# The expert stage of an encoder block on one core, with its weight conversion pipelined by a step

## The chip, the cores and the metric

The kernel runs on one core of one Trainium2 chip. The metric is the device time of one execution in microseconds (us), lower being better. Engines are named as in the profile: PE multiplies matrices (PEld is its weight load), ACT and DVE are the scalar and the vector engine, POOL is GpSimd, SP issues most DMAs.

## What is computed

The block normalizes its input, runs a convolution branch and a bidirectional state-space branch, merges them, and adds a mixture of experts in which each of the 16 experts picks its 130 tokens. The change touches the mixture alone:

```python
def expert_choice_ffn(xn, w_router, w_gate, w_up, w_down):
    b, T, d = xn.shape                                   # 1, 1040, 1024
    cap = CAPACITY_FACTOR * T // N_EXPERTS               # 130
    aff = jax.nn.softmax(jnp.einsum('btd,de->bte', xn, w_router).astype(jnp.float32), axis=-1)
    top_aff, top_idx = lax.top_k(jnp.swapaxes(aff, 1, 2), cap)
    bi = jnp.arange(b)[:, None, None]
    xg = xn[bi, top_idx]
    hg = jnp.einsum('becd,edf->becf', xg, w_gate)        # w_gate, w_up: 16 x 1024 x 2048
    hu = jnp.einsum('becd,edf->becf', xg, w_up)
    y = jnp.einsum('becf,efd->becd', jax.nn.silu(hg) * hu, w_down)   # w_down: 16 x 2048 x 1024
    y = y * top_aff[..., None].astype(y.dtype)
    return jnp.zeros_like(xn).at[bi, top_idx].add(y)
```

## The kernel before

The expert stage is the last third of the program. It goes through 16 experts `e` in 4 steps `q` each, 64 steps in all. A step makes 512 of the 2048 hidden columns. It needs four weight tiles of 1 MB in float32, two of the gate (`m` = 0, halves `b` of the contraction) and two of the up matrix (`m` = 1), which `load_gu` (L898) brings into the pool `ring`; all of `ring`'s tiles are named `wst`.

The two products are made in float16 pieces. Per step `gate_up` does this:

- ACT squares the four tiles and sums each row (L912). The squares themselves are not used; they are written into the tile that is to hold `wl`. The sums go to `sq`.
- `scales` (L874 to L888) turns the sums into a power of two for each matrix: DVE rounds `sq` (`sqb`, L877), PE adds it over the partitions with two tiny products (L880), DVE makes the scales `sc` (L883 to L887).
- The weights are split: `wh` is the tile times its scale in float16, by ACT for `b` = 0 (L917) and by DVE for `b` = 1 (L918); `wl` is what `wh` leaves over, all four by DVE (L920). `wh` and `wl` live in the pool `split`.
- `pair(0)` and `pair(1)` each make 96 matmuls (`mm3`, L96 to L98: `wh` times the two pieces of the tokens `xT`, and `wl` times the first), then `sil` on ACT (L939) and `ac` on DVE (L941).

In the same step the previous expert's down product goes on: `bring` (L949) loads two tiles of `w_down` of 1 MB, and each `down` (L963) makes 16 float32 products of 8 column blocks out of one (in the profile 32 matmuls). After an expert's eighth `down` its result is copied (`yT`, L970), turned back by 16 transposes (L978), scaled (`yo`, L979) and added to memory by four indirect DMAs of POOL (L980): `put`. For the next expert, `Route` makes a one-hot table (L825), the list of tokens (`idx`, L837), gathers them with two indirect DMAs (L841), and `turn` transposes them (L869) into `xT` (ACT, L871). The first two steps of expert 0 take float32 weights (L931), and during the first experts `select` searches the threshold of the others.

The order on each engine comes out of a scheduler that takes the program's order as a priority; `high_priority(offset=...)` puts a piece ahead by so many instructions. All engines run their own list in order. A tile of a pool can be filled again when its last reader is through: `ring` has 10 tiles, `split` 8 `wh` and 8 `wl` (two steps' worth of four each), PSUM's `rp`, which the turns, the transposes of `put` and the norm product share, has two. The loads stand on SP in the order in which the program asks for them: gate and up of the next step, then the two down tiles of this one.

## Time and profile before

| what | us |
|---|---|
| median of 3 runs (lowest, highest) | 3150.16 (3142.86, 3152.40) |
| profiled execution | 3151.71 |
| its span | 3149.90 |
| PE busy | 2867.0 |
| DVE busy | 2208.8 |
| ACT busy | 1575.6 |
| POOL busy | 757.0 |
| expert steps, 1762.4 to 3085.3 of the span | 1322.9 |
| of these twelve experts, 1983.4 to 3011.2 | 1027.8 |

PE is busy in nine tenths of the span, but a busy PE can run at a lower clock: the column PEclk of the windows view is the clock that was granted, 1.00 being the upper one of two levels (2.4 GHz) and 0.50 the lower (1.2 GHz). So PE loses time in two ways, by standing idle and by a clock below 1.00, and both are read per stretch. A line in brackets in the waits and the timeline is the idle time before an instruction and what ended it. The DMA share is the busy share of the core's 16 DMA engines; it reads up to 1.05 where they are full.

### The profile page before, as it was taken

To read this page: it belongs to the slowest core of one execution; us is meant where nothing else is said; L and a number is where in the kernel's file an instruction comes from. 1 tells how busy PE (TensorE), PEld (TensorE's weight loads), DVE (VectorE), ACT (ScalarE), POOL (GpSimd) and SP (SyncE) were. 2 spreads that over 40 slices of the span, in tenths; PEclk is the share of its full clock that TensorE was granted. 3 is DMA by queue.
4 is the path that set the end of the run, shared out by engine and by line. 5 is a ranking of instruction groups with operands and counts; after the bars stand their busy time and mean duration, and the time that the engine had idled before them with its cause. 6 is when DMAs were issued, how large, how long until landed. Compare 5 with 4: busy or idle time off the path is not lost. (4 is left out here: it accounts for less than half of the span.)

```text
span 3149.9 us, 65509 instructions
## 1 busy us (share of the span) xinstructions
PE 2867.0 (91%) x28079; PEld 2716.6 (86%) x28079; DVE 2208.8 (70%) x2703; ACT 1575.6 (50%) x2351; POOL 757.0 (24%) x661
## 2 busy tenths in 40 slices
PE   8999999886987989899997888999999999999996
PEld 7999999776776778889966888999998999999996
DVE  7967769396896886897455766677776666666683
ACT  4423333443646464443222665665665656556653
POOL 1101011253454544330000003222222222221123
PEclk9999999898999899999998999999999999999998
DMA  4324233677768776524345778989888888888995
GB/s 119 108 91 136 78 119 104 170 140 197 142 198 164 205 162 157 173 61 133 119 135 204 265 272 294 319 312 331 304 303 287 306 297 308 305 310 307 318 341 161
DMA packets 425971, 665.99 MB, mean 211 GB/s; under 512 B 29217, under 2 KB 213953, under 8 KB 425673
## 3 DMA queue, kind: packets, MB, share of 16 engines
q1 hardware_dynamic: 366032, 514.83, 51.7%
q0 software_dynamic: 25760, 73.27, 7.6%
q10 hardware_dynamic: 33888, 73.71, 7.3%
q8 instruction: 220, 3.60, 0.5%
q14 instruction: 71, 0.58, 0.1%
HBM read 585.15 MB, written 76.59 MB: 210 GB/s over the span
## 5 line engine op out<-in xcount | busy, mean ns | idle before, releaser
L98 PE MATMUL gu<-xT,wl 128*128 128x130 f16 x3968 | 710.8, 223 | 50.4 <-DVE wl L920 50.4
L96 PE MATMUL gu<-xT,wh 128*128 128x130 f16 x3968 | 718.4, 226 | 17.6 <-ACT wh L917 15.5
L97 PE MATMUL gu<-xT,wh 128*128 128x130 f16 x3968 | 717.3, 223 | 0.0
L96 PE MATMUL mm<-uh,wh 128*128 128x346 f32 (+2 forms) x1752 | 583.9, 333 | 21.3 <-ACT wh L151 18.6
L97 PE MATMUL mm<-ul,wh 128*128 128x346 f32 (+2 forms) x1752 | 580.3, 331 | 0.3 <-DVE ul L187 0.3
L98 PE MATMUL mm<-uh,wl 128*128 128x346 f32 (+2 forms) x1752 | 579.2, 332 | 0.0
L920 DVE SCALAR_TENSOR_TENSOR wl<-wst,sc,wh 128x2048 f16<-128x2048 f32 x248 | 569.6, 2344 | 0.0
L912 ACT ACTIVATE wl<-wst 128x2048 bf16<-128x2048 f32 x248 | 470.5, 1899 | 180.0 <-PE gu L98 168.2
L963 PE MATMUL dn<-ac,wst 128*128 128x130 f32 x3840 | 473.7, 279 | 11.3 <-DMA wst<-in_w_exp_down_dram 11.2
L963 PEld LDWEIGHTS dn<-ac,wst 128*128 128x128 f32 x3840 | 447.1, 192 | 14.9 <-DMA wst<-in_w_exp_down_dram 14.9
L98 PEld LDWEIGHTS <-wl 128*128 128x128 f16 x3968 | 390.3, 99 | 54.8 <-DVE wl L920 54.8
L96 PEld LDWEIGHTS <-wh 128*128 128x128 f16 x3968 | 393.2, 99 | 20.7 <-ACT wh L917 20.1
L97 PEld LDWEIGHTS <-wh 128*128 128x128 f16 x3968 | 399.4, 101 | 3.3 <-issue 2.1
L96 PEld LDWEIGHTS mm<-uh,wh 128*128 128x128 f32 x1752 | 337.1, 192 | 36.6 <-ACT wh L151 20.2
L97 PEld LDWEIGHTS mm<-ul,wh 128*128 128x128 f32 x1752 | 337.1, 192 | 12.7 <-issue 11.7
L98 PEld LDWEIGHTS mm<-uh,wl 128*128 128x128 f32 x1752 | 336.3, 192 | 10.8 <-issue 10.4
L235 DVE SCALAR_TENSOR_TENSOR co<-ci,cp,co 128x1040 f32<-128x1040 f32 x240 | 344.1, 1434 | 1.7
L841 POOL DMA_INDIRECT xg<-hn_d,idx x32 | 151.2, 4725 | 767.9 <-DVE wgt L845 726.4
L917 ACT ACTIVATE wh<-wst,sc 128x2048 f16<-128x2048 f32 x124 | 241.4, 1994 | 88.7 <-DVE sc L885 74.8
L428 ACT ACTIVATE E<-row,cst 128x128 f32<-128x128 f32 (+1 forms) x576 | 170.1, 378 | 200.3 <-DMA row<-cs_d 162.9
L420 POOL TENSOR_TENSOR xw<-xk,dtw 128x512 f32<-128x512 f32 (+1 forms) x136 | 189.3, 1397 | 178.8 <-DMA xk<-xk_d 74.6
L151 ACT ACTIVATE wh<-wr 128x1024 fp32r<-128x1024 f32 (+1 forms) x113 | 105.6, 934 | 243.6 <-PE mm L97 194.4
(329 smaller groups left out, 4642.0 us busy)
## 6 DMA issues: line engine op xcount, KB each, us to landing
wst<-in_w_exp_gate_dram SPq DMA_DIRECT2D x128, 1024.0 KB, 8.2
wst<-in_w_exp_up_dram SPq DMA_DIRECT2D x128, 1024.0 KB, 10.4
wst<-in_w_exp_down_dram SPq DMA_DIRECT2D x128, 1024.0 KB, 7.9
wr<-in_w_in_dram SPq DMA_DIRECT2D x73, 512.0 KB, 4.4
row<-cs_d SPq DMA_DIRECT2D x64, 512.0 KB, 10.3
xk<-xk_d ACTq DMA_DIRECT2D x64, 256.0 KB, 6.3
xbc_d<-po POOLq DMA_DIRECT2D x24, 520.0 KB, 3.2
xk_d<-xt POOLq DMA_DIRECT2D x20, 512.0 KB, 3.9
```

The costliest lines, as they stand in the source:

```text
L96: pe.matmul(ps, wh(k), xh(k), start=(k == 0), stop=False)
L97: pe.matmul(ps, wh(k), xl(k), start=False, stop=False)
L98: pe.matmul(ps, wl(k), xh(k), start=False, stop=(k == K - 1))
L151: act.activation(out=wh[:, :K], in_=r, func=AF.Copy)
L235: dve.scalar_tensor_tensor(co, ci[:, m:m + T], cp[:, j, m:m + 1], co, op0=OP.mult, op1=OP.add)
L420: pool.tensor_mul(heads(o[:L]), heads(xk[:L]), dtw[:L, c, w, hs].unsqueeze(2).to_broadcast([L, HG, 64]))
L428: act.activation(out=E[:L, j, :L], in_=row[:L, j, :L], func=AF.Relu, scale=-1.0, bias=cs)
L841: self.got = nc.gpsimd.indirect_dma_start(out=xg.rearrange("p a d -> p (a d)"), out_offset=None, in_=hn_d.rearrange("t a d -> t (a d)"), i ...
L912: act.activation(out=wl[m][b].bitcast(BF), in_=t[m][b], func=AF.Square, accum_out=sq[:, b, m:m + 1])
L917: act.activation(out=wh[m][0], in_=t[m][0], func=AF.Copy, scale=sc[:, 1, m:m + 1])
L920: dve.scalar_tensor_tensor(wl[m][b], t[m][b], sc[:, 1, m:m + 1], wh[m][b], op0=OP.mult, op1=OP.subtract)
L963: pe.matmul(last["dn"][b // 3][:, b % 3], t[:, k, b * P:b * P + P], ac[:, 2 * i + k], start=(i + k == 0 and b % 3 == 0), stop=(i == 7 and ...
```

## The change

- The squares go into one tile of their own, `junk` (L762), which nobody reads, and no longer into `wl`. They are a function of their own, `norms`.
- Scales and split of step n+1 (`convert`) stand in the middle of step n, between its first `down` and its second pair. The scales' priority offset falls from 1500 to 150. A step's `gate_up` takes the finished tiles.
- Gate and up tiles are asked for two steps ahead and no longer one (`RUN`), after the step's two down tiles and no longer before them.
- `ring` has 11 tiles, not 10; `wh` has 7, not 8; `wl` has 6, not 8.
- `sil` and `ac` get a priority offset of 300, `yo` too.
- `put` is a generator: the first half of the result's columns starts at the end of the expert's last step and goes on after the next step's first pair, the second after its second pair.
- The next expert's `route` stands in step 1, no longer in step 0 (expert 2's was there already).

```diff
@@ -34,9 +34,9 @@
 NR = 2
 NS = NE - NR
 PRE = 2
-RUN = 1
+RUN = 2
 NATIVE = (0, 1)
-SELECT, LATE = 1, 1
+SELECT = 1
 NCH = [(0, 348), (348, 346), (694, 346)]
 NCH0 = [(0, 272), (272, 384), (656, 384)]
 OFF_Z, OFF_XBC, OFF_DT, OFF_GATE = 2048, 4096, 7168, 7232
@@ -754,11 +754,12 @@
     HC = CAP // 2
     mstack, rings, splits, fins = ExitStack(), ExitStack(), ExitStack(), ExitStack()
     with mstack:
-        ring = rings.enter_context(tpool("ring", bufs=10, side="right"))
-        split = splits.enter_context(tpool("split", bufs=8, side="right"))
+        ring = rings.enter_context(tpool("ring", bufs=11, side="right"))
+        split = splits.enter_context(tpool("split", bufs=7, side="right"))
         go = mstack.enter_context(tpool("go", bufs=2))
         mo = mstack.enter_context(tpool("mo", bufs=2))
         sel = mstack.enter_context(tpool("sel"))
+        junk = sel.tile([P, 4, 512], BF, name="junk")
         mps2 = mstack.enter_context(tpool("mps2", bufs=2, space=PSUM))
 
         def every(t):
@@ -900,25 +901,35 @@
                     ts.append(t)
             return ts[:2], ts[2:]
 
+        def norms(t):
+
+            sq = go.tile([P, 2, 2], F32, name="sq")
+            for m in range(2):
+                for b in range(2):
+                    act.activation(out=junk, in_=t[m][b], func=AF.Square,
+                                   accum_out=sq[:, b, m:m + 1])
+            return sq
+
+        def convert(t, sq):
+
+            with tc.high_priority(offset=150):
+                sc = scales(sq, sx[:, 0:1])
+            wh = [[split.tile([P, 4, 512], F16, name="wh") for _ in range(2)] for _ in range(2)]
+            wl = [[split.tile([P, 4, 512], F16, name="wl", bufs=6) for _ in range(2)] for _ in range(2)]
+            for m in range(2):
+                act.activation(out=wh[m][0], in_=t[m][0], func=AF.Copy, scale=sc[:, 1, m:m + 1])
+                dve.tensor_scalar_mul(wh[m][1], t[m][1], sc[:, 1, m:m + 1])
+                for b in (1, 0):
+                    dve.scalar_tensor_tensor(wl[m][b], t[m][b], sc[:, 1, m:m + 1], wh[m][b], op0=OP.mult,
+                                             op1=OP.subtract)
+            return wh, wl, sc
+
         def gate_up(t, q, xT, ac, first=None):
+
 
             native = first and q in NATIVE
             if not native:
-                wh = [[split.tile([P, 4, 512], F16, name="wh") for _ in range(2)] for _ in range(2)]
-                wl = [[split.tile([P, 4, 512], F16, name="wl") for _ in range(2)] for _ in range(2)]
-                sq = go.tile([P, 2, 2], F32, name="sq")
-                for m in range(2):
-                    for b in range(2):
-                        act.activation(out=wl[m][b].bitcast(BF), in_=t[m][b], func=AF.Square,
-                                       accum_out=sq[:, b, m:m + 1])
-                with tc.high_priority(offset=1500):
-                    sc = scales(sq, sx[:, 0:1])
-                for m in range(2):
-                    act.activation(out=wh[m][0], in_=t[m][0], func=AF.Copy, scale=sc[:, 1, m:m + 1])
-                    dve.tensor_scalar_mul(wh[m][1], t[m][1], sc[:, 1, m:m + 1])
-                    for b in (1, 0):
-                        dve.scalar_tensor_tensor(wl[m][b], t[m][b], sc[:, 1, m:m + 1], wh[m][b], op0=OP.mult,
-                                                 op1=OP.subtract)
+                wh, wl, sc = t
 
             def pair(p):
                 pss = []
@@ -934,11 +945,12 @@
                             mm3(ps[:, f], lambda k: wh[m][k // 4][:, k % 4, cols], lambda k: wl[m][k // 4][:, k % 4, cols],
                                 lambda k: xT[0][:, k], lambda k: xT[1][:, k], KD)
                     pss.append(ps)
-                sil = mo.tile([P, 2, CAP], F32, name="sil")
                 s0, s1 = (sx[:, 0:1], sx[:, 0:1]) if native else (sc[:, 2, 0:1], sc[:, 2, 1:2])
-                act.activation(out=sil, in_=pss[0], func=AF.Silu, scale=s0)
                 b0 = 4 * q + 2 * p
-                dve.scalar_tensor_tensor(ac[:, b0:b0 + 2], pss[1], s1, sil, op0=OP.mult, op1=OP.mult)
+                with tc.high_priority(offset=300):
+                    sil = mo.tile([P, 2, CAP], F32, name="sil")
+                    act.activation(out=sil, in_=pss[0], func=AF.Silu, scale=s0)
+                    dve.scalar_tensor_tensor(ac[:, b0:b0 + 2], pss[1], s1, sil, op0=OP.mult, op1=OP.mult)
 
             return pair
 
@@ -971,12 +983,14 @@
 
         def put(r):
             for b in range(2):
+                yield
                 yo = mo.tile([HC, 2, 512], F32, name=f"yo{b}", bufs=1)
                 for h in range(2):
                     ps = mps2.tile([HC, 4, P], F32, name="rp")
                     for j in range(4):
                         pe.transpose(ps[:, j], last["yT"][:, 4 * b + j, HC * h:HC * h + HC], ident)
-                    dve.tensor_scalar_mul(yo[:, h], ps, r.wgt[:, h:h + 1])
+                    with tc.high_priority(offset=300):
+                        dve.tensor_scalar_mul(yo[:, h], ps, r.wgt[:, h:h + 1])
                     nc.gpsimd.indirect_dma_start(out=h2_d[b], in_=yo[:, h], in_offset=None,
                                                  compute_op=OP.add,
                                                  out_offset=bass.IndirectOffsetOnAxis(ap=r.idx[:, h:h + 1], axis=0),
@@ -1029,37 +1043,55 @@
             cur, prev = route(0), None
             cur.whole()
             cur.turn()
-        done = None
-        for e in range(NE):
-            ac = mo.tile([P, 16, CAP], F32, name="ac")
-            for q in range(4):
-                for _ in range(2 if (e, q) >= (0, SELECT) else 0):
-                    next(finding, None)
-                if e + 1 < NE and q == (LATE if e + 1 == NR else 0):
-                    for _ in finding if e + 1 == NR else ():
-                        pass
-                    with tc.high_priority(offset=1500) if e + 1 == NR else nullcontext():
-                        nxt = route(e + 1)
-                while loads and loads[0] <= (e + (q + RUN) // 4, (q + RUN) % 4):
-                    e2, q2 = loads.pop(0)
-                    with tc.issue_after(stored.ins) if e2 == 0 and q2 >= 1 else nullcontext():
-                        tiles[e2, q2] = load_gu(e2, q2, cur.xgs[1] if e2 == 0 else None)
-                ds = [bring(e - 1, 2 * q + i) for i in range(2)] if prev else []
-                pair = gate_up(tiles.pop((e, q)), q, cur.xT, ac, None if e else cur)
-                for i in range(2):
-                    pair(i)
-                    if i == 0 and done:
-                        put(done)
-                        done = None
-                    if prev:
-                        down(2 * q + i, ds[i], prev[0])
-                if e + 1 < NE and q == 2:
-                    nxt.turn()
+        done = iter(())
+        steps = [(e, q) for e in range(NE) for q in range(4)]
+        ready = {}
+
+        def load_next(n):
+            while loads and loads[0] in steps[:n + RUN + 1]:
+                e2, q2 = loads.pop(0)
+                with tc.issue_after(stored.ins) if e2 == 0 and q2 >= 1 else nullcontext():
+                    tiles[e2, q2] = load_gu(e2, q2, cur.xgs[1] if e2 == 0 else None)
+
+        for n, (e, q) in enumerate(steps):
+            if q == 0:
+                ac = mo.tile([P, 16, CAP], F32, name="ac")
+            for _ in range(2 if (e, q) >= (0, SELECT) else 0):
+                next(finding, None)
+            if e + 1 < NE and q == 1:
+                for _ in finding if e + 1 == NR else ():
+                    pass
+                with tc.high_priority(offset=1500) if e + 1 == NR else nullcontext():
+                    nxt = route(e + 1)
             if prev:
-                done = prev[1]
-            prev = (ac, cur)
-            cur = nxt if e + 1 < NE else cur
-        put(done)
+                ds = [bring(e - 1, 2 * q + i) for i in range(2)]
+            load_next(n)
+            coming = steps[n + 1] if n + 1 < len(steps) else None
+            raw = tiles.pop(coming) if coming and (coming[0] or coming[1] not in NATIVE) else None
+            if raw:
+                sq = norms(raw)
+            pair = gate_up(ready.pop((e, q)) if (e, q) in ready else tiles.pop((e, q)), q, cur.xT, ac,
+                           None if e else cur)
+            pair(0)
+            next(done, None)
+            if prev:
+                down(2 * q, ds[0], prev[0])
+            if raw:
+                ready[coming] = convert(raw, sq)
+            pair(1)
+            next(done, None)
+            if prev:
+                down(2 * q + 1, ds[1], prev[0])
+            if e + 1 < NE and q == 2:
+                nxt.turn()
+            if q == 3:
+                if prev:
+                    done = put(prev[1])
+                    next(done)
+                prev = (ac, cur)
+                cur = nxt if e + 1 < NE else cur
+        for _ in done:
+            pass
         for b in range(2):
             t = mo.tile([HC, 2, 512], F32, name=f"yo{b}", bufs=1)
             for h in range(2):
```

On ACT, in an expert's third step, where the next expert's tokens are turned, this stood before (`sil` and `xT` as above; `wl_...,sq_...<-wst_...` is a square, `wh` a conversion; a name's number tells one tile from the next):

```order
L939 ACTIVATE sil_22136<-gu_22038,sc_22024 128x260
L912 ACTIVATE wl_22642,sq_22646<-wst_22314 128x2048
L939 ACTIVATE sil_22253<-gu_22155,sc_22024 128x260
L912 ACTIVATE wl_22643,sq_22646<-wst_22316 128x2048
L912 ACTIVATE wl_22644,sq_22646<-wst_22318 128x2048
L912 ACTIVATE wl_22645,sq_22646<-wst_22320 128x2048
L871 ACTIVATE xT0_22272<-rp_22274 128x520
L871 ACTIVATE xT0_22272<-rp_22284 128x520
L871 ACTIVATE xT1_22273<-rp_22294 128x520
L871 ACTIVATE xT1_22273<-rp_22304 128x520
L970 ACTIVATE yT_22592<-dn_21580 128x390
L917 ACTIVATE wh_22326<-wst_21994,sc_22344 128x2048
```

All squares of one step are ahead of the turn there, and the conversion `wh` behind it and behind `yT`. On the same engine at the turn this stands now:

```order
L952 ACTIVATE sil_23371<-gu_23273,sc_23117 128x260
L909 ACTIVATE junk_15341,sq_23588<-wst_23264 128x2048
L909 ACTIVATE junk_15341,sq_23588<-wst_23266 128x2048
L952 ACTIVATE sil_23515<-gu_23417,sc_23117 128x260
L909 ACTIVATE junk_15341,sq_23871<-wst_23580 128x2048
L872 ACTIVATE xT0_23534<-rp_23536 128x520
L872 ACTIVATE xT0_23534<-rp_23546 128x520
L909 ACTIVATE junk_15341,sq_23871<-wst_23582 128x2048
L872 ACTIVATE xT1_23535<-rp_23556 128x520
L872 ACTIVATE xT1_23535<-rp_23566 128x520
L952 ACTIVATE sil_23691<-gu_23593,sc_23395 128x260
L909 ACTIVATE junk_15341,sq_23871<-wst_23584 128x2048
```

Squares of the next tiles (`sq_23871`, two steps ahead of the products) stand ahead of and between the turn's two halves, and no conversion follows at once.

On DVE, at the border between two experts, this stood before (`wl` the split, `sc` the scales, `oh`, `idx` and `wgt` the next expert's route):

```order
L918 TENSOR_SCALAR wh_21106<-wst_20775,sc_21123 128x2048
L918 TENSOR_SCALAR wh_21108<-wst_20779,sc_21123 128x2048
L887 TENSOR_SCALAR sc_21123<-sc_21123,sx_96 128x2
L883 TENSOR_SCALAR sc_21435<-rp_21432 128x2
L837 TENSOR_REDUCE idx_21397<-rp_21378 65x2
L845 TENSOR_REDUCE wgt_21398<-rp_21378 65x2
L825 TENSOR_TENSOR oh_22597<-iot_100,slot_95 128x1170
L920 SCALAR_TENSOR_TENSOR wl_21110<-wst_20775,sc_21123,wh_21106 128x2048
L920 SCALAR_TENSOR_TENSOR wl_21109<-wst_20773,sc_21123,wh_21105 128x2048
L920 SCALAR_TENSOR_TENSOR wl_21112<-wst_20779,sc_21123,wh_21108 128x2048
L884 TENSOR_SCALAR sc_21435<-sc_21435 128x2
L920 SCALAR_TENSOR_TENSOR wl_21111<-wst_20777,sc_21123,wh_21107 128x2048
```

A whole step's conversion and the route stand in one row, with the next step's scales among them. On DVE at the same border this stands now:

```order
L921 TENSOR_SCALAR wh_21280<-wst_20820,sc_21273 128x2048
L888 TENSOR_SCALAR sc_21273<-sc_21273,sx_96 128x2
L953 SCALAR_TENSOR_TENSOR ac_20195<-gu_21200,sc_20953,sil_21249 128x260
L923 SCALAR_TENSOR_TENSOR wl_21284<-wst_20820,sc_21273,wh_21280 128x2048
L923 SCALAR_TENSOR_TENSOR wl_21283<-wst_20818,sc_21273,wh_21279 128x2048
L878 CAST sqb_21569<-sq_21429 128x4
L921 TENSOR_SCALAR wh_21282<-wst_20824,sc_21273 128x2048
L923 SCALAR_TENSOR_TENSOR wl_21286<-wst_20824,sc_21273,wh_21282 128x2048
L923 SCALAR_TENSOR_TENSOR wl_21285<-wst_20822,sc_21273,wh_21281 128x2048
L953 SCALAR_TENSOR_TENSOR ac_20195<-gu_21344,sc_20953,sil_21393 128x260
```

The conversion for the coming step (`sc_21273`) stands between the results `ac` of the running one (`sc_20953`), and the rounding of the sums of the step after it (`sq_21429`) stands between the conversion's two halves, `m` = 0 and `m` = 1.

## Rows read from the trace of the kernel before

**Rows 1.** The page: busy time, share of the span and instructions of each engine.

```profile
PE 2867.0 (91%) x28079; PEld 2716.6 (86%) x28079; DVE 2208.8 (70%) x2703; ACT 1575.6 (50%) x2351; POOL 757.0 (24%) x661
```

**Rows 2.** Windows view, expert stage and tail; its head line names the columns.

```profile
core 0: us, PE busy (x) PEld busy (x) DVE busy (x) ACT busy (x) POOL busy (x), PEclk, DMA share, GB/s
1762.40:1894.10 131.70, 116.10 (x1716) 113.77 (x1714) 94.88 (x159) 82.93 (x87) 8.47 (x4) 0.94 0.80 285
1894.10:1983.40 89.30, 80.26 (x1073) 78.12 (x1071) 61.37 (x65) 48.20 (x50) 31.13 (x8) 0.92 0.88 301
1983.40:3011.20 1027.80, 961.70 (x13157) 944.20 (x13155) 673.85 (x754) 632.42 (x663) 224.25 (x70) 0.96 0.88 308
3085.30:3149.90 64.60, 36.03 (x288) 34.85 (x286) 23.62 (x44) 22.41 (x77) 24.54 (x18) 0.79 0.50 155
```

**Rows 3.** Windows view, same columns: one expert, in four pieces (three shown) and whole.

```profile
2518.60:2536.90 18.30, 18.30 (x260) 18.27 (x258) 15.19 (x16) 12.71 (x13) 0.00 (x0) 1.00 1.03 379
2536.90:2566.20 29.30, 28.10 (x376) 27.57 (x374) 3.88 (x10) 14.33 (x19) 0.00 (x0) 1.00 0.68 233
2566.20:2585.40 19.20, 14.52 (x204) 13.71 (x205) 19.20 (x20) 9.58 (x10) 12.39 (x3) 0.82 0.84 271
2499.80:2585.40 85.60, 79.72 (x1100) 78.30 (x1099) 56.12 (x64) 52.29 (x56) 18.67 (x6) 0.96 0.87 303
```

**Rows 4.** Waits, twelve experts: engine, line, waited for, us in total, times, longest.

```profile
PE gu L98 <- DVE wl L920: 43.7, 12, 3.9
PE gu L96 <- ACT wh L917: 11.0, 23, 1.6
DVE sc L883 <- PE rp L880: 116.2, 36, 9.6
```

**Rows 5.** Timeline of PE at an expert's border: start, us, instruction, [idle before <- releaser].

```profile
2572.85 0.29 PE L98 MATMUL gu<-xT,wl 128*128 128x130 f16 x1 [3.92 <-DVE wl L920]
2573.26 0.32 PE L96 MATMUL gu<-xT,wh 128*128 128x130 f16 x1
2576.32 0.22 PE L96 MATMUL gu<-xT,wh 128*128 128x130 f16 x1
```

**Rows 6.** Timeline of ACT and DVE, one border earlier.

```profile
2477.69 0.16 DVE L883 TENSOR_SCALAR sc<-rp 128x2 f32<-128x2 f32 x1 [6.45 <-PE rp L880]
2482.32 4.60 DVE L920 SCALAR_TENSOR_TENSOR wl<-wst,sc,wh 128x2048 f16<-128x2048 f32 x2
```

**Rows 7.** Groups by line, twelve experts: xcount | busy us, mean ns | idle before.

```profile
L912 ACT ACTIVATE wl<-wst 128x2048 bf16<-128x2048 f32 x194 | 367.9, 1898 | 134.1 <-PE gu L98 134.1
L918 DVE TENSOR_SCALAR wh<-wst,sc 128x2048 f16<-128x2048 f32 x96 | 119.2, 1283 | 0.0
L920 DVE SCALAR_TENSOR_TENSOR wl<-wst,sc,wh 128x2048 f16<-128x2048 f32 x192 | 441.1, 2344 | 0.0
L871 ACT ACTIVATE xT<-rp 128x520 f16<-128x520 f16 x48 | 26.1, 594 | 26.3 <-PE rp L869 26.3
```

**Rows 8.** DMA view, twelve experts: MB moved; issues: xcount, KB, median us to landing.

```profile
DMA packets 134329, 316.22 MB, mean 308 GB/s; under 512 B 6767, under 2 KB 6767, under 8 KB 134205
wst<-in_w_exp_up_dram SPq DMA_DIRECT2D x96, 1024.0 KB, 10.6
```

**Rows 9.** DMA view, 2459 to 2474.7: the same for tiles that come alone.

```profile
wst<-in_w_exp_down_dram SPq DMA_DIRECT2D x2, 1024.0 KB, 4.9
```

**Rows 10.** Windows view, as rows 2: transfers at their fullest, without and with gathers.

```profile
2443.00:2458.00 15.00, 15.00 (x227) 14.99 (x225) 7.83 (x6) 8.52 (x10) 0.00 (x0) 1.00 1.04 391
2404.00:2434.00 30.00, 30.00 (x446) 29.93 (x444) 29.13 (x29) 23.65 (x23) 11.86 (x6) 0.98 1.03 349
```

**Rows 11.** Timeline of PE: 22 down matmuls behind a gap, in two experts.

```profile
2387.95 4.38 PE L963 MATMUL dn<-ac,wst 128*128 128x130 f32 x22 [1.62 <-DMA wst<-in_w_exp_down_dram]
2817.09 2.73 PE L963 MATMUL dn<-ac,wst 128*128 128x130 f32 x22 [0.82 <-DMA wst<-in_w_exp_down_dram]
```

**Rows 12.** Windows view, as rows 2: expert 2's tokens are waited for.

```profile
1829.00:1837.00 8.00, 1.05 (x12) 0.47 (x9) 7.93 (x16) 6.02 (x4) 4.30 (x2) 0.69 0.64 198
```

## The prediction

> **What bounds the kernel now.** The page comes first: PE is busy for 91% of the span, DVE for 70% and ACT for half [rows 1]. Time can only be won where PE stands or runs at its lower clock, so the next view is PE's busy time and granted clock by stage [rows 2]. In the twelve experts from 1983.4 to 3011.2, 85.65 us each, PE is idle for 1027.8 - 961.7 = 66.1 us, and the clock of 0.96 costs another 0.04 x 1027.8 = 41.1: together 107.2, or 8.93 per expert. The stretch before it loses 9.0 + 7.1 = 16.2 in the same way, the first experts 15.6 + 7.9 = 23.5. In all that is 147 us. The tail from 3085 on is idle for much of its time too, but it is one chain of down products and stores which the diff doesn't touch.
>
> Where in an expert does the loss sit? The pieces of one expert tell it [rows 3]: two steps pass with PE full at clock 1.00, the long third piece is nearly full, and the fourth, the 19.2 us from the border to the next expert, holds 4.7 us of idle PE and a clock of 0.82. The waits name it [rows 4]: PE waits for `wl` from DVE (43.7 us in 12 waits, one per expert) and for `wh` from ACT (11.0). The timeline shows the price of one: 3.92 us of idle, and behind it matmuls at the lower clock, 0.32 instead of 0.22 us each, until 2576 [rows 5].
>
> Why does the conversion come late? DVE waits 6.45 us for the tiny norm product on PE [rows 6], and 116.2 us in all [rows 4]. PE runs its list in order and gets to that product only when the step's matmuls are done, so scales, `wh` and the first `wl` (until 2487) begin when PE has nothing left to do. It is a latency, made of order; no engine is short of time.
>
> **The change part by part.** *Norm product, scales and split in mid-step.* This removes the cause. The norm product now stands before the running step's second pair, and 192 matmuls plus 64 products of `down` cover the conversion. It needs per step 2 x 1.28 + 4 x 2.34 = 11.9 us on DVE [rows 7], and a step of PE is 18.3 us [rows 3]. If all loss at the borders went, an expert would take 85.65 - 8.93 = 76.7 us; that is PE's floor, since no matmul is removed or added.
>
> *Loads two steps ahead, ring of 11.* Six tiles of 1 MB per step go through the ring as before. The last up tile of the step after next is loaded into a place that the second half of this step's conversion frees. Twelve experts move 316.2 MB, 26.35 each [rows 8]. At the fullest rate of 391 GB/s that takes 67.4 us, at the 349 of a stretch with gathers 75.5 [rows 10]. Both are below 76.7, so DMA isn't the bound by itself, but it is close: 88 to 98% of PE's floor.
>
> *What may be late next.* ACT works in order, and squares of tiles that have been asked for two steps ahead now stand in front of and between the halves of the turn. PE's second half of transposes needs `rp` back, hence ACT's first copies, hence the landing of those tiles. From the end of the conversion's first half, which frees the place, to PE's second half there are about 14 us: the second pair and a down, an estimate from the 18.3 us step. The chain needs 4.9 us for a tile that comes alone [rows 9] to 10.6 in a queue [rows 8], a square of 1.9 and two copies of 0.59 [rows 7]: 8 to 13.7, and up to 4 us more if gathers are among the transfers (the rate then falls from 391 to 349 [rows 10], a tenth of the step's 18 us makes 2; twice that as the end). So PE waits between 0 and 4 us per expert; I take 1.5, since the lone landing is the nearer row where queues stand two steps ahead. Such a gap sits at the edge of what touches the clock: behind an idle of 1.62 us the next 22 matmuls took 4.38 us, behind one of 0.82 us 2.73 [rows 11]. So 1.65 us are added, or nothing; I take 1.7. Together 3.2 us per expert stay.
>
> *The same order on DVE.* The rounding of the sums for the step after next stands between the two halves of a conversion. It waits for ACT's last square, hence for the last up tile. That makes a loop: last `wl` frees the place, the tile lands (4.9 to 10.6), square 1.9, then rounding, `wh` 1.28 and two `wl` of 2.34 [rows 7], 7.9 us behind the landing and with the short operations about 8.3. It takes 13 to 19 us per step, against PE's 18.3. The upper end just touches the step. I put it at no cost, with the upper end (0.6 us x 4, or 2.4 per expert) in the range.
>
> *What stays.* Expert 2's tokens are gathered only when the threshold search is done. PE then has 7 us of 8 idle [rows 12]; with half of that stage's clock loss (4) that is 11 to 12 us, which the change doesn't reach, since that route stays where it was.
>
> *Edits at no cost.* The tile `junk` makes squares wait for each other, but they are in order on ACT anyway, which is busy for 632 of 1028 us [rows 2]; bound 0 to 1 us per step, taken as 0. `put` in halves issues the same 16 transposes, four `yo` and four indirect stores. The route a step later leaves the gather a step less: gathers are asked for in the second step and needed at the end of the third, some 20 us later by the pieces [rows 3]; if it were late, some 5 us per expert would come back. Fewer `wh` and `wl` tiles tie a conversion to matmuls that are a step old; cover is PE's own progress. The priorities of `sil` and `ac` can only bring PSUM back earlier: 0, or a gain below 1 us per expert.
>
> *Sum.* 147 us are lost now. There stay 13 x 3.2 = 41.6 (twelve experts and the one before) and 12 of the gather: 54. The gain is 93, and the profiled run of 3151.7 becomes 3058.5. The median of the runs is 1.5 below that run: 3057.
>
> **The rivals.** *PE's floor.* If the new waits never show, an expert takes 76.7 to 78 us, and 12 to 12 + 13 x 1.3 = 29 stay: 3015 to 3032. For it speaks that lone tiles land in 4.9 us and that ACT and DVE have a third of their time free; against it that transfers then run at 88% or more, where nothing is lone.
>
> *Transfers become the bound.* In the third piece of an expert the DMA share falls to 0.68 [rows 3]: this slack is what a faster PE uses up. If the queues run at 349 GB/s throughout and each expert still has 6.5 to 9.5 us in which no place is free (now the third piece has 0.32 x 29.3 = 9.4), an expert takes 82 to 85 us, and 69 + 12 to 108 + 12 us stay: 3084 to 3123. Here the Trainium skill speaks against the change: "DMA: Bandwidth & Descriptors", section Specifications and the one on where 436 GB/s comes from, says that between HBM and SBUF the limit of about 358 GB/s per core binds. By that figure 26.35 MB take 73.6 us, which leaves 3 us under the floor for every interruption. The trace disagrees, with 391 GB/s over 15 us [rows 10], and the Trainium skill's own figure there for a core that streams alone, 425 GB/s, is above it too.
>
> *The in-order loop is the bound: slower than before.* The loop on DVE costs landing + 8.3 us in each of four steps. Before, a step is 85.65 / 4 = 21.4 us on average; so the change is slower once the last up tile lands more than 13.1 us behind its release. If one more 1 MB tile stands ahead of it in the queue, 10.6 + 4.9 = 15.5 us: a step is 23.8, an expert 95, and 13 x 9.4 = 122 us are added, less some 11 of the first experts: 3261. Against it: the two up tiles are released 2.3 us apart and the gate tiles before, so the queue should be short.
>
> *The wait only moves.* PE waits for `wl` of the second half, or for the turn, as long as it waits for the first now: 85 to 86 us per expert, 3150.
>
> **How the numbers follow.** Expert at 78 to 82 us: 0.55, 3032 to 3084, with 3057 as its value. PE's floor: 0.25. Transfers: 0.08. Only moved: 0.04. Loop: 0.08. About 0.3% or 9.5 us can be told from no change. Faster by more: 0.55 + 0.25 + 0.08 = 0.88; within: 0.04; slower: 0.08. The range leaves out the slower case, the case of no change, a little of the floor's best end and of the transfers' worst: 3012 to 3115.
>
> **What would show it.** Of the changed kernel: the clock of the twelve experts at 0.98 or more, an expert at 78 to 82 us, PE's wait for `wl` near zero, and in its place waits of the transposes of the turn for `xT` of 1 to 3 us per expert. The mean rate should be some 308 x 85.65 / 79.9 = 330 GB/s. The tail should be the same 64.6 us. The prediction is wrong if DVE's rounding waits for squares for more than a few us per step and PE with it (the loop), if PE waits for tiles (transfers), or if no waits are left (floor).

## The result, and the profile after

The changed kernel takes 3057.97 us in the median of 4 runs (3050.98 to 3062.95), the kernel before 3147.75 beside it (4 runs). The ratio is 0.9713, with a 95% interval of 0.9684 to 0.9742: 90 us less. The profiled execution took 3062.95 us, its span is 3061.2.

Section 1 of the page of the changed kernel (compare [rows 1]):

```profile
PE 2830.0 (92%) x28079; PEld 2693.4 (88%) x28079; DVE 2216.2 (72%) x2703; ACT 1578.6 (52%) x2351; POOL 722.2 (24%) x661
```

The windows view of the same kernel, columns as in [rows 2]: the first experts, the same twelve experts as in [rows 2] (from the first product of the fourth expert to that of the last), and the tail, whose window starts 16 matmuls earlier here than in [rows 2]:

```profile
1716.00:1956.10 240.10, 223.32 (x3085) 220.84 (x3083) 176.28 (x280) 157.73 (x164) 24.70 (x10) 0.95 0.87 307
1956.10:2920.80 964.70, 936.39 (x13179) 929.41 (x13178) 680.17 (x757) 632.84 (x661) 206.63 (x72) 0.99 0.95 328
2994.30:3061.20 66.90, 37.09 (x304) 35.92 (x302) 23.63 (x44) 23.35 (x78) 24.58 (x18) 0.79 0.49 150
```

An expert takes 964.7 / 12 = 80.4 us instead of 85.65. PE stands for 28.3 us in all twelve, not 66.1, and its clock is 0.99, not 0.96; the transfers run at 328 GB/s and not at 308.

All that PE waits for in those twelve experts (waits view: us in total, times, longest), against the 43.7 and 11.0 us for `wl` and `wh` of [rows 4]:

```profile
PE rp L870 <- ACT xT L872: 22.7, 12, 3.1
PE rp L881 <- DVE sqb L878: 3.7, 6, 1.0
PE rp L881 <- ACT xT L872: 0.9, 1, 0.9
```

In the waits of the changed kernel no row of PE is left for `wl` or `wh`: the waits at the border of two experts are gone. What is left is the turn: one wait per expert, for the copies `xT`.

Where the 88.7 us between the two spans lie is told by four stretches. The first float32 product of expert 0 starts at 1726.9 us before and at 1716.0 after; behind it come the first experts, the twelve, and the rest:

| stretch | before | after | less by | foretold |
|---|---|---|---|---|
| up to the first float32 product of expert 0 | 1726.9 | 1716.0 | 10.9 | 0 |
| from there to the fourth expert | 256.5 | 240.1 | 16.4 | 24.5 |
| twelve experts | 1027.8 | 964.7 | 63.1 | 68.8 |
| the rest | 138.7 | 140.4 | -1.7 | 0 |
| span | 3149.9 | 3061.2 | 88.7 | 93.3 |

### The profile page after: what moved, and what is told of

The parts are those of the page before. It is cut to its first block, busy times and chain, and to the rows that moved or that the text cites. A ratio compares the mean times of both kernels' runs of the same rounds, so it can differ in the third digit from the quotient of the medians.

```text
span 3061.2 us, 65630 instructions
## 1 busy us (share of the span) xinstructions
PE 2830.0 (92%) x28079; PEld 2693.4 (88%) x28079; DVE 2216.2 (72%) x2703; ACT 1578.6 (52%) x2351; POOL 722.2 (24%) x661
## 5 line engine op out<-in xcount | busy, mean ns | idle before, releaser
L96 PE MATMUL gu<-xT,wh 128*128 128x130 f16 x3968 | 703.9, 223 | 4.3 <-ACT sil L952 3.8
L97 PE MATMUL gu<-xT,wh 128*128 128x130 f16 x3968 | 703.5, 221 | 0.0
L98 PE MATMUL gu<-xT,wl 128*128 128x130 f16 x3968 | 702.8, 221 | 0.6 <-DVE wl L923 0.4
L909 ACT ACTIVATE junk<-wst 128x2048 bf16<-128x2048 f32 x248 | 473.7, 1910 | 388.8 <-DMA wst<-in_w_exp_gate_dram 311.9
L975 PE MATMUL dn<-ac,wst 128*128 128x130 f32 x3840 | 459.8, 277 | 0.0
L97 PEld LDWEIGHTS <-wh 128*128 128x128 f16 x3968 | 394.4, 99 | 8.3 <-issue 6.8
L994 POOL DMA_INDIRECT h<-yo,idx x60 | 181.7, 3029 | 921.3 <-DVE yo L993 770.6
L96 PEld LDWEIGHTS <-wh 128*128 128x128 f16 x3968 | 388.9, 98 | 2.6 <-ACT wh L920 2.4
L97 PEld LDWEIGHTS mm<-ul,wh 128*128 128x128 f32 x1752 | 336.6, 192 | 12.8 <-issue 11.8
```

Source lines behind the costliest of these rows:

```text
L96: pe.matmul(ps, wh(k), xh(k), start=(k == 0), stop=False)
L97: pe.matmul(ps, wh(k), xl(k), start=False, stop=False)
L98: pe.matmul(ps, wl(k), xh(k), start=False, stop=(k == K - 1))
L909: act.activation(out=junk, in_=t[m][b], func=AF.Square, accum_out=sq[:, b, m:m + 1])
L975: pe.matmul(last["dn"][b // 3][:, b % 3], t[:, k, b * P:b * P + P], ac[:, 2 * i + k], start=(i + k == 0 and b % 3 == 0), stop=(i == 7 and ...
L994: nc.gpsimd.indirect_dma_start(out=h2_d[b], in_=yo[:, h], in_offset=None, compute_op=OP.add, out_offset=bass.IndirectOffsetOnAxis(ap=r.idx ...
```

## Experiments

Each verdict is on an expert's time in the twelve experts, read from a window from the fourth expert's first product to the last expert's, and on the waits of PE in it. The total time of each kernel is compared with the kernel before, run beside it.

### The same kernel again: what the first 10.9 us are

No edit.

> The kernel before, unchanged, in another run. In the two profiles the first float32 products of expert 0 (before L931, after L942) start at 1726.9 us before and at 1716.0 us after, though no instruction ahead of them was changed or stands in another order. If these 10.9 us are a matter of the run (transfers that land a little earlier in the scan part), this run's profile starts them somewhere between 1714 and 1728, not tied to 1726.9; if they come from the change, at 1726 to 1728 again. Total 3140 to 3153 either way.

It took 3147.36 us against 3146.02 (ratio 1.0003, 0.9983 to 1.0023). The groups of the float32 products in expert 0, first in the trace that the prediction read and then in this one (min/median/max ns, first and last start in us):

```profile
L931 PE MATMUL gu<-yT,wst x256: 272/275/564, 1726.9 to 1762.2; 128*128 128x130 f32 x128
```

```profile
L931 PE MATMUL gu<-yT,wst x256: 272/275/567, 1719.8 to 1755.3; 128*128 128x130 f32 x128
```

The same program reaches this point 7.1 us earlier. Over the 14 profiles of this case it lies between 1710.8 and 1726.9, with no order among the kernels. So the 10.9 us of the first line of the table are not shown to be the change's: the part in front of the expert stage varies by as much from run to run, and single totals with it (before: 3137 to 3160 in one series). Counted from this point to the end of the span the kernel before takes 1423.0 us in its one profile and 1423.3 in the other, the changed kernel 1345.2. A difference of 78 us is far beyond such variation.

### The squares kept out of the turn

```diff
-                        act.activation(out=self.xT[i][:, k0:k0 + 4]...
+                        self.copied = act.activation(out=self.xT[i][:, k0:k0 + 4]...
-                sq = norms(raw)
+                with tc.issue_after(cur.copied.ins) if q == 0 else nullcontext():
+                    sq = norms(raw)
```

> The changed kernel, but the squares of the tiles two steps ahead may stand on ACT only behind the four copies of the turn. Theory: the 24.9 us that PE waited for these copies in twelve experts and the lower clock behind them (3.4 us at half speed in 7 of 12) go, 2.1 + 1.0 us per expert: an expert at 77.2 to 78, 13 x 3 = 39 us less than the changed kernel, about 3020 (3010 to 3030). Rival: the squares are late now, rounding and norm product wait for them (PE L881 on DVE's sqb at over 2 us per expert), and the time stays at 3045 to 3065.

3022.54 us (ratio 0.9610, 0.9570 to 0.9650), as the theory said. The twelve experts:

```profile
1955.10:2883.00 927.90, 923.00 (x13179) 918.73 (x13178) 680.32 (x757) 634.12 (x661) 199.96 (x72) 1.00 0.98 341
```

77.3 us each, clock 1.00, no wait for `xT` left, 4.4 us of waiting for the rounding in all. So the turn cost the changed kernel 80.4 - 77.3 = 3.1 us per expert. How it does is seen in ACT's timeline of the changed kernel at one turn (start, us, instruction, [idle before <- releaser]):

```profile
2659.25 1.91 ACT L909 ACTIVATE junk<-wst 128x2048 bf16<-128x2048 f32 x1 [5.43 <-DMA wst<-in_w_exp_gate_dram]
2661.06 0.19 ACT L909 ACTIVATION_READ_ACCUMULATOR junk<-wst 128x1 f32 x1
2661.16 1.08 ACT L872 ACTIVATE xT<-rp 128x520 f16<-128x520 f16 x2
```

and in its chain that ended last, at the same place (start, us, what):

```profile
2645.05 2.35 DVE wl L923
2647.42 11.74 DMA wst<-in_w_exp_gate_dram
2659.25 2.00 ACT junk L909 x2
2661.25 0.99 ACT xT L872 x2
2662.28 0.40 PE rp L870 x8
```

ACT stands for 5.4 us in front of a square whose tile is on its way for 11.7 us, from the `wl` that freed its place. PE's first transposes were done at 2659.2; the copies that would let the next ones run are second in ACT's list. At this turn the tile lands just as the transposes end, and the copies wait for the 1.9 us of the square itself. It is the mildest of the twelve: over all of them the first copy starts 1.9 to 4.1 us after the first transposes have ended. Nothing is slow here. One instruction stands one place too early.

### Result transposes in one piece again

```diff
             pair(0)
-            next(done, None)
+            for _ in done:
+                pass
 ...
             pair(1)
-            next(done, None)
 ...
                     done = put(prev[1])
-                    next(done)
```

> The changed kernel, but put stands in one piece behind the next step's first pair, as before. Theory: the 16 transposes cost PE the same wherever they stand and its results are stored early enough: 3050 to 3066, no difference to the changed kernel. Rival: in one piece they hold rp's two tiles and DVE for four scalings in a row, the norm product and the conversion wait behind them: 1 to 3 us per expert more, 3070 to 3095.

The `next(done)` at an expert's end only brings `put` to its first `yield` and issues nothing: in the changed kernel the two halves stand behind the first and the second pair of the next expert's first step.

3018.93 us (0.9597, 0.9562 to 0.9632): neither theory; undoing this part makes the kernel 39 us faster. Twelve experts:

```profile
1953.40:2878.50 925.10, 922.72 (x13178) 918.36 (x13176) 681.05 (x757) 635.13 (x661) 155.41 (x72) 1.00 0.97 342
```

77.1 us each. ACT at a turn of this kernel:

```profile
2628.79 1.10 ACT L872 ACTIVATE xT<-rp 128x520 f16<-128x520 f16 x2 [1.58 <-PE rp L870]
2630.64 1.91 ACT L909 ACTIVATE junk<-wst 128x2048 bf16<-128x2048 f32 x1 [0.76 <-DMA wst<-in_w_exp_gate_dram]
2632.46 0.18 ACT L909 ACTIVATION_READ_ACCUMULATOR junk<-wst 128x1 f32 x1
2632.55 1.08 ACT L872 ACTIVATE xT<-rp 128x520 f16<-128x520 f16 x2
```

The first copies now come first, and ACT waits for PE, not PE for ACT. The edit is far from the turn, but it moved one square behind the copies. Counted from the start, ACT has done 61, 77, 93 squares and so on before the twelve turns of the changed kernel, and 60, 76, 92 here: one fewer each time. With that square out of the way, halves (77.3, the run before) and one piece (77.1) are alike, so the halves themselves bring and cost nothing that shows.

### A ring of ten

```diff
-        ring = rings.enter_context(tpool("ring", bufs=11, side="right"))
+        ring = rings.enter_context(tpool("ring", bufs=10, side="right"))
```

> The changed kernel with a ring of 10 tiles as before instead of 11. Theory: the last up tile still lands in time (a loop of 13 to 19 us per step against PE's 18.3 to 20), the turn waits a little longer: 0 to 2 us per expert more, 3055 to 3085. Rival: with one place less the loop on DVE (a place is freed, the tile lands, is squared, rounded, and only then the second half of the split goes on) closes behind PE in each step: 3100 or more.

3029.19 us (0.9624, 0.9594 to 0.9653), below both. Twelve experts:

```profile
1959.30:2890.60 931.30, 922.93 (x13178) 918.27 (x13176) 680.71 (x757) 638.46 (x661) 156.62 (x72) 1.00 0.97 340
```

77.6 us. As in the run before, one square fewer stands ahead of each turn (60, 76, 92 and so on), and no transpose waits for a copy; what PE still waits for is the norm product's place in `rp`, 8.2 us in all. The eleventh place alone buys nothing that shows.

### Loads one step ahead

```diff
-RUN = 2
+RUN = 1
```

> The changed kernel, but gate and up tiles are asked for one step ahead instead of two (behind the same step's down tiles). Theory: the order of the conversion brought the gain, and the ring's 11 places are used in a circle, so a place is free equally early; PE's wait for wl stays under 5 us in twelve experts, an expert takes 80 to 82 us, 3050 to 3075 in all. Rival: the lead of two steps brought it; squares and so scales come late in every step, PE waits for the norm product or for wh and wl, an expert takes 84 us or more, over 3110.

3028.98 us (0.9628, 0.9593 to 0.9662): below what either theory gave. An expert takes 79.2 us. The wait for `xT` is gone here too, and another takes its place:

```profile
DVE sqb L878 <- ACT junk L909: 24.1, 12, 3.0
PE rp L881 <- DVE sqb L878: 20.6, 10, 3.1
```

This is the loop of the prediction: the rounding waits for a square, the square for its tile, and PE's norm product for the rounding, 1.7 us per expert. So the second step of lead is worth 79.2 - 77.3 = 1.9 us per expert once the turn is free. This kernel's first experts take 228.7 us, 11 less than the changed kernel's; why stays open.

### All three undone together

```diff
-RUN = 2
+RUN = 1
```

with the ring of ten and `put` in one piece, as above.

> Own tile and mid-step conversion kept, and of the changed kernel three parts undone together: loads one step ahead, ring of 10 tiles, put in one piece. Theory: each of the three alone gained time by moving a square out of the turn; without any of them an expert takes 77 to 79.5 us, 3010 to 3035. Rival: the lead and the eleventh place are needed as soon as both are missing; tiles come late, rounding waits for squares and PE's norm product for rounding by more than 3 us per expert: 82 us or more, 3070 and up.

3040.63 us (0.9671, 0.9648 to 0.9694), an expert at 78.9, and PE waits in the loop for 14.7 us in twelve. An expert is inside the theory's span, the median 6 us above it. So lead, ring and halves are not what brought the gain: without them the kernel is at least as fast as with them. What is left of the change is the own tile, the mid-step conversion, the priorities, the smaller number of `wh` and `wl` tiles, the later route and the down tiles ahead of gate and up in SP's list. The first three have runs of their own below; the last three were not undone by themselves.

### The squares in `wl` again

```diff
+            wl = [[split.tile([P, 4, 512], F16, name="wl") for _ in range(2)] for _ in range(2)]
...
-                    act.activation(out=junk, in_=t[m][b], func=AF.Square,
+                    act.activation(out=wl[m][b].bitcast(BF), in_=t[m][b], func=AF.Square,
```

> The changed kernel, but the squares are written into the tiles of wl again, as before, and the 4 KB of the tile of their own go to a seventh wl. Theory: a square then waits until PE is through with the wl that lay there, which with 7 tiles is in the running step; scales and split fall behind it and PE waits for wl again, 3 to 7 us per expert: 3095 to 3150. Rival: ACT has time enough to square late, and the mid-step order alone brought the gain: 3050 to 3070.

3242.45 us (1.0325, 1.0279 to 1.0370): the theory was right in kind, but its price was far too small, for this is slower than before. An expert takes 92.3 us, and the wait is there in every step, not once per expert:

```profile
ACT wl L909 <- PE gu L98: 167.4, 41, 4.5
PE gu L98 <- DVE wl L922: 105.4, 48, 3.7
```

The squares of the next step wait until PE leaves `wl`; scales and split follow them, and PE meets the end of that chain 48 times.

### The own tile alone, in the kernel before

```diff
+        junk = sel.tile([P, 4, 512], BF, name="junk")
...
-                    act.activation(out=wl[m][b].bitcast(BF), in_=t[m][b], func=AF.Square,
+                    act.activation(out=junk, in_=t[m][b], func=AF.Square,
```

> The kernel before with one part of the change alone: the squares go into a tile of their own (its 4 KB come from an eighth wh). Theory: the late wl at the border of two experts comes from the place of norm product and conversion in the lists of PE and DVE, which this leaves as they were; ACT no longer waits for PE before its squares (134 us in twelve experts before), but nobody waited for those squares: 3135 to 3155, an expert at 85 to 86. Rival: the own tile is the part that counts, since undoing it in the changed kernel cost 184 us; an expert at 82 us or less, under 3105.

3147.63 us against 3144.79 (1.0012, 0.9991 to 1.0032), an expert at 86.2. (The room for the tile is taken from `wh`, which has seven.) ACT no longer waits for PE before its squares, only for their tiles, and the border waits stay: PE for `wl` 33.2 us in the twelve experts and for `wh` 19.5. The tile is a condition of the mid-step conversion, as the run before shows, and no gain by itself.

### The conversion at the end of a step again

```diff
-            if raw:
-                ready[coming] = convert(raw, sq)
             pair(1)
             next(done, None)
             if prev:
                 down(2 * q + 1, ds[1], prev[0])
+            if raw:
+                ready[coming] = convert(raw, sq)
```

> The changed kernel with one thing undone: a step's scales and split stand at the end of the step before (behind its second down) and no longer in its middle; the squares keep their own tile, the loads their lead. Theory: the place of the conversion brought nearly all of the gain in the expert steps. The norm product falls behind the matmuls of a step again, at the border of two experts a whole conversion stands in one row, and PE waits some 4 us for wl there and runs 7 us at the lower clock: an expert at 84.5 to 86, 3115 to 3150 in all. Rival: the own tile and the lead of the loads brought it; an expert stays at 80 to 82, 3050 to 3070.

3087.45 us (0.9815, 0.9781 to 0.9849): between the two. An expert takes 82.2 us, with the turn out of the way. PE's wait in twelve experts:

```profile
PE dn L975 <- DMA wst<-in_w_exp_down_dram: 32.2, 12, 3.9
```

PE doesn't wait for `wl`, as the theory had it, but for down tiles. That a late split gives back the ring's places late, so that the down tile of the next step is loaded late, would explain it; this is argued, not shown. Against the kernels with a free turn the place in mid-step is worth 82.2 - 77.3 = 4.9 us per expert, 64 us in thirteen. The kernel before takes 85.65: the other 3.4 us per expert are gained even with the conversion at the end of a step, and which of the remaining edits brings them stays open.

### Priorities as before

```diff
-            with tc.high_priority(offset=150):
+            with tc.high_priority(offset=1500):
                 sc = scales(sq, sx[:, 0:1])
...
-                with tc.high_priority(offset=300):
+                with nullcontext():
                     sil = mo.tile([P, 2, CAP], F32, name="sil")
```

and the same for `yo`.

> The changed kernel with the priorities of before (scales 1500 ahead, sil, ac and yo none); two squares stand ahead of and in the turn as in the changed kernel. Theory: the priorities decide nothing, the turn costs PE 2 us and the clock behind it 1 us per expert again: 3045 to 3070, an expert at 80 to 81. Rival: without them sil and ac stand behind squares and conversions, PE waits for gu's place in PSUM: 3080 or more.

3049.44 us (0.9699, 0.9655 to 0.9744), an expert at 80.2, PE waiting 19.2 us for `xT` in the twelve turns, with as many squares ahead of each as in the changed kernel: the changed kernel again, its turn included. The priorities decide nothing that shows.

### The first experts: the search earlier

On the kernel with the squares out of the turn:

```diff
-            for _ in range(2 if (e, q) >= (0, SELECT) else 0):
+            for _ in range(3 if (e, q) >= (0, SELECT) else 0):
...
-            if e + 1 < NE and q == 1:
+            if e + 1 < NE and q == (0 if e + 1 == NR else 1):
```

> The kernel of the run before (squares behind the turn) with the threshold search of the first experts in three rounds per step instead of two, and expert 2's route one step earlier. Theory: PE's 7.8 us of waiting for expert 2's tokens and the lower clock behind it (6.7 us at half speed) are there because the search ends late; a step earlier it goes: 8 to 12 us less, 3010 to 3016. Rival: three rounds per step push the split of the first steps back on DVE, PE waits for wh and wl there, and the time stays at 3018 to 3030.

3024.63 us (0.9616, 0.9582 to 0.9650), the rival. The wait for expert 2's tokens is gone; PE waits in the same stretch for `wh` (6.7 us) and `wl` (4.5). The first experts take 236.6 us, against 234.5 with the squares out of the turn alone.

The other way, with `put` in one piece, the squares out of the turn, and only the second edit:

> The fastest of the kernels so far (put in one piece) with the squares two steps ahead behind the turn, and expert 2's route one step earlier; the search keeps two rounds per step, what is left of it is run at once. Theory: PE's 7.5 us of waiting for expert 2's tokens shrink by half or more, the split of the first steps is hardly pushed back: an expert at 77 us, 3005 to 3015. Rival: the rounds that are run at once push the split of the first steps back on DVE, as in the run with three rounds per step, and the gain goes there: 3015 to 3030.

3014.66 us (0.9603, 0.9555 to 0.9651). Twelve experts:

```profile
1949.20:2870.90 921.70, 921.67 (x13178) 918.15 (x13176) 681.27 (x757) 635.47 (x661) 157.78 (x72) 1.00 0.97 344
```

PE is not idle at all, 76.8 us per expert. The total is just inside the theory's range, but not for its reason: the first experts take 235.5 us, against 232.8 with `put` in one piece alone, and PE waits there for `wh` (5.0 us), `wl` (2.8) and `sil` (2.8) in place of the tokens. The earlier route gives nothing. This is the fastest kernel of the case, though it can't be told from that with `put` alone (3018.93); its profile reached the first product at 1713.7, early in the spread.

## Why the prediction came out as it did

*The border: right.* That the late conversion is a matter of order holds: with the place in mid-step the waits of 43.7 and 11.0 us are gone, and moved back it costs 4.9 us per expert. That it comes back as a wait for down tiles was not foreseen. The norm product as the cause inside that order is read from [rows 4] to [rows 6] and not shown by a run of its own: DVE's wait for it is 116.2 us before, 73.9 in the changed kernel and 168.9 with the conversion moved back, but also 129.1 with the ring of ten, where PE stands for 8.4 us in all twelve experts. So that wait alone doesn't cost PE time. The floor of 76.7 us is 76.8 to 77.3 in the runs.

*The turn: right in place, its size in part by luck.* 3.2 us per expert were foretold as 1.5 of idle and 1.7 of clock; it is 22.7 / 12 = 1.9 of idle, and a lower clock behind 6 of 12 turns. Free of the turn an expert takes 3.1 us less. The 14 us of room hold: from the end of the `wl` that frees the place to the moment PE is ready for the second half are 12.8 to 14.2 us in the twelve turns. The landing doesn't: it was put nearer to 4.9 us than to 10.6, with up to 4 more for gathers as the end, and takes 11.7 to 14.7 from that `wl`. With 4.9 the prediction's own chain is 8 us long and leaves no wait at all; its 1.5 was a choice between 0 and 4 that the reason given for it doesn't support. And the clock's 1.7 was counted at every turn, where half of them show it.

*The loop at no cost: right here.* PE's wait for the rounding is 3.7 us in twelve experts. With loads one step ahead it is 20.6.

*Transfers.* They were called close to the bound, at 88 to 98% of the floor. In the fastest kernel the DMA engines are busy for 97% at 344 GB/s while PE has no gap, so both ends meet. The Trainium skill ("DMA: Bandwidth & Descriptors", Specifications and the section on where 436 GB/s comes from) puts the limit at about 358 GB/s per core between HBM and SBUF. No mean over twelve experts goes higher, but a 20 us window of the changed kernel does:

```profile
2620.00:2640.40 20.40, 19.53 (x281) 19.21 (x279) 17.84 (x18) 13.55 (x13) 12.88 (x4) 1.00 1.02 365
```

With the 391 GB/s of [rows 10] the trace speaks against that figure as a limit here.

*What stays: mis-sized.* 12 us of waiting for expert 2's tokens were to stay as they were. Seen from the first float32 product the gather is issued later now: at 1829.67 - 1726.9 = 102.8 us before, at 1831.40 - 1716.0 = 115.4 after. POOL's timeline of the changed kernel:

```profile
1831.40 2.84 POOL L842 DMA_INDIRECT xg<-hn_d,idx  x1 [94.38 <-DVE sc L884]
```

The steps around that wait and the one ahead of them, in the windows view:

```profile
1751.50:1799.90 48.40, 43.68 (x687) 42.98 (x685) 40.74 (x87) 37.72 (x41) 0.00 (x0) 0.96 0.92 344
1799.90:1857.00 57.10, 47.29 (x686) 46.34 (x687) 41.49 (x66) 31.20 (x32) 4.42 (x2) 0.88 0.74 261
```

The second loses 9.8 us idle and 0.12 x 57.1 = 6.9 by the clock, 16.7 instead of 12; the first still loses 4.7 and 1.9, of which the sum kept nothing. These 4.7 and 6.6 us are more than the 8.1 us by which the first experts fell short of 24.5. The search shares DVE with conversions that now come earlier; that this delays it is argued, not shown, but both attempts to bring it forward only moved the wait, to `wh` and `wl` above all.

*Edits at no cost: wrong for the changed kernel.* `put` in halves and the ring were put at nothing, by their own work, and that holds (77.1 and 77.6 us without them). But each also moves instructions in the scheduler's list, and with all of them the kernel has one square more in front of the turn. The step that failed is the one that took the order at the turn as a given and asked only for the price of the wait; it did not ask which edits hold it there. Undoing any one of three edits gave 29 to 39 us in the medians; counted from the first float32 product, the profiles take 1318.3 us with loads one step ahead, 1306.4 with the ring of ten and 1297.5 with `put` in one piece, against 1345.2.

*The total: nearer than its parts, by luck.* 3057 was forecast and 3057.97 measured. In the profiles the expert stage gave 16.4 + 63.1 - 1.7 = 78 us, not 93: 8.1 too little in the first experts, 5.7 in the twelve, 1.7 in the rest. The other 10.9 lie in front of it, where no instruction was changed, and make up for most of that. How much of the 90 us between the medians is of that kind stays open.

## What to carry over

When stages are pipelined through in-order lists, ask of every instruction that now runs ahead what stands behind it: a square whose tile was 11.7 us on its way held a 0.6 us copy, and PE with it. An edit that costs nothing by its own work can still move a neighbour by one place, so try each part of a change alone: leaving out any one of three parts made this kernel 29 to 39 us faster, leaving out all three 17. Before a difference of 10 us is given to a change, see how much the unchanged part of the program moves between runs (16 us here).

## What the runs showed of the hardware

The length of a gap does not settle whether PE's clock falls behind it. In the changed kernel's timeline a turn with a gap of 1.69 us,

```profile
2741.41 0.90 PE L870 MATMUL rp<-identh,xg 65*128 65x65 f16 x16 [1.69 <-ACT xT L872]
```

is followed by a lower clock (0.92 on average from 2737.9 to 2760.4), and one of 2.29 us

```profile
2822.53 0.90 PE L870 MATMUL rp<-identh,xg 65*128 65x65 f16 x16 [2.29 <-ACT xT L872]
```

is not (1.00 from 2818.4 to 2839.9), with the same kinds of matmuls around both. At another turn a gap of the same length as the second,

```profile
2018.92 1.09 PE L870 MATMUL rp<-identh,xg 65*128 65x65 f16 x16 [2.29 <-ACT xT L872]
```

is followed by the lower clock (0.92 from 2014.3 to 2036.0). The two gaps of [rows 11] suggested a border between 0.82 and 1.62 us; there is none so simple.
